# Second layer's attention of a two-layer decoder: scores in one run, projections in four parts, transposes and values in two shared PSUM banks

## Chip, cores and metric

The kernel runs on one core of a Trainium2 chip. The metric is the device time of one execution in microseconds (us), shown as the median of several runs. TensorE (PE) multiplies, with weight loads listed apart (PEld); VectorE (DVE) and ScalarE (ACT) read and write its results in PSUM, which has 8 banks of 2 KB a partition; SyncE (SP) and GpSimd (POOL) issue DMAs.

## What is computed

512 tokens of width 1024 go through two layers. The first mixes by a gated delta rule; the second, which the change touches, by attention over a sliding window of 128 tokens, with 12 query heads, 2 shared key/value heads of width 64 and a sink logit for each head. In both layers 4 further heads attend to 256 memory tokens. Then come the output projection and a gated feed-forward part (swiglu). Cut to the second layer:

```
h = rms_norm(x, ln_mix[layer])
proj = h @ swa_w_q[bl]                              # 1024 -> 768 + 256
q = apply_partial_rope(proj[..., :SWA_Q_W].reshape(b_sz, s_len, SWA_HEADS, SWA_DH), cos, sin)
mix_out = sliding_window_attention(q, shared_k, shared_v, swa_sinks[bl])
mem_q = proj[..., SWA_Q_W:]
mem_o = memory_attention(mem_q.reshape(b_sz, s_len, MEM_HEADS, MEM_DH), mem_k, mem_v)
x = x + jnp.concatenate([mix_out, mem_o], axis=-1) @ w_out[layer]
x = x + swiglu(rms_norm(x, ln_ffn[layer]), w_gate_up[layer], w_down[layer])

# in sliding_window_attention, over blocks of 128 queries and 2 x 128 keys:
m = jnp.maximum(jnp.max(s, axis=-1, keepdims=True), sink)
p = jnp.exp(s - m)
p = p / (jnp.sum(p, axis=-1, keepdims=True) + jnp.exp(sink - m))
o = jnp.einsum("bnhgqk,bnkhd->bnqhgd", p, vw)
```

## The kernel before

**Layout.** Activations lie transposed: 8 tiles of 128 features x 512 tokens. A projection (project, L198) makes one such tile from 8. Each operand is split into a high and a low part in fp32r (split, L165: hi by ScalarE, the rest lo by VectorE), and mm3 (L190) adds three products hi x hi, hi x lo, lo x hi for each of the 8 pieces k: 24 matmuls of 512 columns in one PSUM bank, all from L143, the helper line of every matmul. L137 is ScalarE's copy, L150 VectorE's tensor_tensor, L147 the transposes. weight (L179) loads a 128x1024 weight tile into wraw (2 buffers) and splits it into whi and wlo (3 buffers each).

**The second layer's attention** (swa, L1085). Query tiles 0 to 5 hold two heads each, on partitions 0 to 63 and 64 to 127; tiles 6 and 7 hold the four memory heads. A tile passes through these steps:
- queries(t): a projection, in a bank of pj, then a rotation by VectorE (rope, L1076) into q (3 buffers), or a product with rstd for tiles 6 and 7;
- scores (L723): for each of 4 query blocks n and both heads b, q times keys, on 64 rows of TensorE, into banks of qk. Two blocks share one qk buffer of two banks. VectorE adds the mask and takes the maximum into sm (L747), or for memory tiles takes the maximum (L751), and ScalarE writes the exponentials to sm. These fp32 matmuls appear as two instructions each in the profile, so that a tile has 16, in two halves of 8; so do the value matmuls;
- weigh (L759): for query tiles the sink and the exponentials first (L769 to L780), then the reciprocal of the sums, then for each block n: scaling (VectorE for even n, ScalarE for odd n), transposes into a bank of pt, a copy to pf or pfm (VectorE for n = 2, else ScalarE), and after the fourth block all products with the values into the bank sc, on 64 columns of TensorE;
- split (L825): that bank to the pair mix[t], h by ScalarE and l by VectorE.

PSUM in this stage has pj=2 banks, g=1, qk=1 buffer of two banks, pt=2, sc=1.

**Order.** swa writes out: queries 6 and 7, keys, values, scores of 6, the values' transposes, queries 0, scores of 7; then for t from 0 to 5 queries(t+1), scores of t, and weigh of the tile two behind; then weigh of 4 and 5. output (L828) follows: eight output tiles ("rows") m, each a projection over mix in the order k = 6, 7, 0, ..., 5, in banks pj, pj, g in turn, then by VectorE the addition to x (L837), a new pair of x times gain (L839: ScalarE, then VectorE) and a square for the next norm (L841).

A scheduler turns this into one list for each engine before the run: whenever an engine is free it takes the first instruction in program order whose inputs and buffers are ready by its own model of time, so that later instructions can be drawn ahead. nosync (L113) adds an order that costs no semaphore: the first transposes after a scores step stand behind its last matmul (L799), and the first value matmul behind the last transpose (L822). The list is fixed; on the chip each engine keeps to it and waits.

Of the kernel before, what the change touches and what calls it, by code (L numbers as in the profile page):

```python
# [18 lines left out]
P = 128  # L19
T = 512  # L20
D = 1024
KD = D // P
# [63 lines left out]
class Builder:  # L86
    def __init__(self, tc, a):
        self.tc, self.nc, self.a = tc, tc.nc, a
        self.n = 0
        self.table, self.table_ins, self.table_users = None, None, []  # L90


# [17 lines left out]
    def bank(self, tag, shape=(P, T)):  # L110
        return self.t(self.pp, list(shape), F32, tag, self.pbufs[tag])
# [114 lines left out]
    def build(self):  # L226
        tc, nc, a = self.tc, self.nc, self.a
        with ExitStack() as st:
            opened = lambda name, **kw: tc.tile_pool(name=name, bufs=1, reuse_waits="tile", **kw)
            pool = lambda name, **kw: st.enter_context(opened(name, **kw))  # L230
            cp = pool("const")
            self.wpool, self.apool = pool("w"), pool("acta")
            self.dpool = pool("scratch", space=DRAM)
            self.load_constants(cp)
            self.weng = nc.vector
            with opened("layer0", side="right") as self.mpool:
                with self.banks(pj=3, g=2, sc=3):
                    with opened("early", side="right") as ep:
                        self.mem_and_norm(ep)
                        self.gates(ep)  # L240
                    with opened("gdn", side="right") as gp:
                        mix = self.gdn(gp)
                    self.bpool, xp = pool("actb"), pool("x")
                    self.x = [self.t(xp, [P, T], F32, f"x{k}") for k in range(KD)]
                    for k in range(KD):
                        nc.sync.dma_start(self.x[k], a["xT"][:, k, :])
                    self.rstd, self.cosT, self.sinT = (self.t(xp, [P, T], F32, n) for n in ("rstd", "cosT", "sinT"))
                    h = self.output(xp, 0, mix, self.bpool)
            with opened("ffn0", side="right") as fp, self.banks(pj=2, g=6):
                self.ffn(fp, xp, 0, h, self.apool, rope=True)  # L250
            with self.banks(pj=2, g=1, qk=1, pt=2, sc=1):
                with opened("swa", side="right") as sp:
                    mix = self.swa(sp)
                h = self.output(xp, 1, mix, self.apool)
            with opened("ffn1", side="right") as fp, self.banks(pj=2, g=6):
                self.ffn(fp, xp, 1, h, self.bpool)

# [465 lines left out]
    def scores(self, pool, q, kk, win):  # L723

        nc = self.nc
        own = "pt" in self.pbufs
        half = [slice(0, 64), slice(64, P)]
        sm = [self.t(pool, [P, 2, 2, 2 * P], F32, "sm", 6 if own else 2) for _ in range(2)]
        sm = [t[:, n] for t in sm for n in range(2)]
        mx, den, nm = (self.t(pool, [P, 2 * NC], F32, t, 3 if own else 2) for t in ("mx", "den", "nm"))  # L730
        for n0 in range(0, NC, 2):
            if own:
                two = self.bank("qk", [P, 2, 2, 2 * P])
                ps = [two[:, b] for b in range(2)]
            else:
                ps = [self.bank("sc" if n0 else "g", [P, 2, 2 * P]) for _ in range(2)]
            for n in (n0, n0 + 1):
                ks = slice((n - 1) * P if n else 0, (n + 1) * P) if win else slice(0, ML)
                c0 = P if win and n == 0 else 0
                for b in range(2):  # L740
                    self.ahead = self.mm(ps[b][:, n - n0, c0:], q[half[b], n * P:(n + 1) * P], kk[half[b], ks])
            for b in range(2):
                i = b * NC + n0
                if win:
                    for n in (n0, n0 + 1):
                        c0 = 0 if n else P
                        nc.vector.tensor_tensor_reduce(  # L747
                            out=sm[n][:, b, c0:], in0=ps[b][:, n - n0, c0:], in1=self.band[:, c0:], scale=1.0,
                            scalar=NEG, op0=ALU.add, op1=ALU.max, accum_out=mx[:, b * NC + n:b * NC + n + 1])
                else:  # L750
                    nc.vector.tensor_reduce(out=mx[:, i:i + 2], in_=ps[b], op=ALU.max, axis=AX.X)  # L751
                    self.ts(nm[:, i:i + 2], mx[:, i:i + 2], -0.125, ALU.mult)
                    for n in (n0, n0 + 1):
                        i = b * NC + n
                        self.fn(sm[n][:, b, :], ps[b][:, n - n0, :], AF.Exp, scale=0.125, bias=nm[:, i:i + 1],
                                accum_out=den[:, i:i + 1])
        return sm, mx, den, nm

    def weigh(self, pool, scores, vv, m, out, sinks):  # L759

        nc = self.nc
        win = sinks is not None
        own = "pt" in self.pbufs
        half = [slice(0, 64), slice(64, P)]
        sm, mx, den, nm = scores
        if win:
            sk = sinks.unsqueeze(2).to_broadcast([P, 2, NC])
# [11 lines left out]
                            accum_out=den[:, i:i + 1])  # L779
            self.tt(nc.vector, den, den, es, ALU.add)  # L780
        nc.vector.reciprocal(den, den)
        o = self.bank("sc")
        group = NC if own else 2
        for n in range(NC):
            if n % group == 0:
# [22 lines left out]
            if own and n == 2:  # L808
                nc.vector.tensor_copy(to, pt[:, k0:])
            else:  # L810
                self.copy(to, pt[:, k0:])
            if (n + 1) % group:
                continue
            if win:
                parts = [(t[:, j, b, :], vv[n - 1 + j][:, half[b]], slice(n * P, (n + 1) * P), j if n else 0, j, b)
                         for n, t in pf.items() for j in range(0 if n else 1, 2) for b in range(2)]
            else:
                parts = [(pf[:, j, b, :], vv[j][:, m * P + 64 * b:m * P + 64 * b + 64],
                          slice((n + 1 - group) * P, (n + 1) * P), j, j, b) for j in range(2) for b in range(2)]
            for t, v, s, first, last, b in parts:  # L820
                ins = self.mm(o[half[b], s], v, t, first == 0, last == 1)
                if turned is not None:  # L822
                    self.nosync(ins, turned)
                    turned = None
        self.split(o, *out)  # L825


    def output(self, xp, layer, mix, hpool):  # L828

        nc, a = self.nc, self.a  # L830
        self.weng = nc.vector
        h = []
        self.acc = None
        for m in range(KD):
            ps = self.project(a["wout"][layer, m], mix, ("pj", "pj", "g")[m % 3],
                              (6, 7, 0, 1, 2, 3, 4, 5))
            self.tt(nc.vector, self.x[m], ps, self.x[m], ALU.add)  # L837
            hl = self.pair(hpool)
            self.split_gain(self.x[m], self.gain(G_FFN[layer], m), *hl)  # L839
            h.append(hl)  # L840
            self.acc = self.accumulate(xp, self.acc, self.x[m], m)  # L841
        return h
# [189 lines left out]

    def rstd_from(self, acc, t=slice(0, T)):
        self.use(LN_EXP)
        ps = self.bank("g")[:, t]
        self.mm(ps, self.ones, acc)
        self.rsqrt(self.rstd[:, t], ps, D)

# [46 lines left out]
    def swa(self, sp):  # L1085
        nc, a = self.nc, self.a
# [7 lines left out]
        kk, vv = [], []  # L1094

        def queries(t):
            ps = self.project(a["wq"][t], h)
            if len(qs) == 0:
                self.rstd_from(self.acc)
                for table in (self.cosT, self.sinT):  # L1100
# [16 lines left out]

        def transpose_values():
            v = vv.pop()
            pt = self.bank("g")  # L1120
            for c in range(NC):
                self.tr(pt[:, c * P:(c + 1) * P], v[:, c * P:(c + 1) * P])
            vt = self.t(sp, [P, NC, P], F32, "vt")
# [3 lines left out]
        def score(t):  # L1127
            got[t] = self.scores(sp, qs[t], kk[0] if t < 6 else memK[t - 6], t < 6)

        def weigh(t):  # L1130
            mix[t] = self.pair(self.bpool)
            if t < 6:
                self.weigh(sp, got[t], vv, t, mix[t], sinks[:, t, :])
            else:
                self.weigh(sp, got[t], memV, t - 6, mix[t], None)

        got = {}
        queries(6)
        queries(7)
        keys()  # L1140
        values()
        score(6)
        transpose_values()
        queries(0)
        score(7)

        behind = [6, 7]
        for t in range(6):
            if t < 5:
                queries(t + 1)  # L1150
            score(t)
            behind.append(t)
            weigh(behind.pop(0))
        for t in behind:
            weigh(t)
        return [mix[t] for t in range(KD)]

    def final(self, fp, squares, t):

# [84 lines left out]
```

## Time and profile before

| | |
|---|---|
| device time, median of 3 runs | 1167.67 us (1167.38 to 1167.92) |
| the profiled execution, its own time | 1167.76 us |
| its span, first to last instruction | 1165.5 us |
| mean granted TensorE clock | 0.998 |
| VectorE, ScalarE busy, whole span | 72%, 54% |
| DMA, mean | 130 GB/s, 151.20 MB |

All times are of one profiled execution, in us from its span's start. A timeline row holds start, duration, engine, line, operation, output<-inputs, shapes and count; equal neighbours are merged, so that "1.14 ... x8" are eight instructions from the first start to the last end. "64*128" means 64 rows and 128 columns of TensorE in use. A bracket gives the engine's idle time ahead and what ended it. Matmuls overlap, so a duration (0.39 for 512 columns) is longer than the distance between two starts, and TensorE counts as busy in between. A row of stretches holds the stretch, its length, the busy time and count of PE, PEld, DVE, ACT and POOL, the granted clock, the share of DMA and GB/s. A group row holds count | busy us, mean ns | idle us before, with who ended it.

The second layer's attention lies at about 660 to 775, its output rows behind it up to about 809.

### The profile page before, as it was taken

The numbers are of one execution on the slowest core, as the hardware profiler recorded it, in microseconds if no ns is written. First come the engines' busy times: TensorE is split into PE (matmuls) and PEld (weight loads), VectorE is DVE, ScalarE is ACT, GpSimd is POOL, SyncE is SP. The second block draws the span as 40 slices with busy tenths as digits, with TensorE's granted clock in tenths as the row PEclk, the third lists the DMA queues.
The fourth block names the chain that finished last, engine by engine and source line by source line (L and its number), as shares of the span: only waits on it lengthen the run. The fifth ranks groups of instructions, "written<-read, shape, count | busy, mean of one in ns | idle before, by whom it ended". The sixth has DMA issues, their size and how long they took to land.

```text
span 1165.5 us, 19274 instructions
## 1 busy us (share of the span) xinstructions
PE 1144.4 (98%) x7330; PEld 994.5 (85%) x7330; DVE 834.7 (72%) x1558; ACT 629.7 (54%) x1250; POOL 83.0 (7%) x93
## 2 busy tenths in 40 slices
PE   7999999999999999999999999999999999999997
PEld 5878777877899998899998876688999988999986
DVE  5664877767788877488966767758788734889644
ACT  7569663366466642266643546865566422566433
POOL 0210000000101101011100000010011000111000
PEclk9999999999999999999999999999999999999999
DMA  8334441224557636367623421144477633676232
GB/s 307 116 109 116 133 126 65 91 91 164 178 129 176 178 103 169 114 167 183 158 76 99 137 74 55 37 116 120 103 181 193 152 100 106 164 187 160 77 100 84
DMA packets 72943, 151.20 MB, mean 130 GB/s; under 512 B 16732, under 2 KB 19444, under 8 KB 72852
## 3 DMA queue, kind: packets, MB, share of 16 engines
q1 hardware_dynamic: 61908, 130.06, 35.3%
q0 software_dynamic: 10944, 19.93, 10.8%
q8 instruction: 57, 0.93, 0.3%
q14 instruction: 34, 0.28, 0.1%
HBM read 143.00 MB, written 6.96 MB: 129 GB/s over the span
## 4 chain that ended last, share of the span: by engine, by line
PE 90%; DVE 4%; ACT 3%; DMA 1%; issue 1%; SPq 0%; DVEq 0%; ACTq 0%
PE pj L143 43%; PE g L143 39%; PE sc L143 6%; ACT sm L131 1%; PE pt L147 1%; DVE wlo L150 1%; PE qk L143 1%; DVE big L150 1%; PE g L147 1%; DMA wraw<-in_wmk 1%; DVE btmp L150 1%; ACT sm L137 1%; DVE qv L153 1%; ACT whi L137 0%; DMA big<-basein 0%
## 5 line engine op out<-in xcount | busy, mean ns | idle before, releaser
L137 ACT ACTIVATE whi<-wraw 128x512 fp32r<-128x512 f32 (+3 forms) x325 | 243.0, 754 | 275.4 <-PE pj L143 173.5
L150 DVE TENSOR_TENSOR wlo<-wraw,whi 128x512 fp32r<-128x512 f32 (+3 forms) x325 | 272.5, 847 | 105.1 <-ACT whi L137 99.6
L143 PE MATMUL pj<-h,whi 128*128 128x512 f32 (+1 forms) x676 | 265.6, 394 | 0.2
L143 PE MATMUL pj<-l,whi 128*128 128x512 f32 (+1 forms) x676 | 265.2, 392 | 0.0
L143 PE MATMUL pj<-h,wlo 128*128 128x512 f32 (+1 forms) x676 | 264.1, 391 | 0.0
L143 PE MATMUL g<-T,whi 128*128 128x256 f32 x1216 | 220.5, 282 | 0.0
L143 PEld LDWEIGHTS g<-T,whi 128*128 128x128 f32 x1216 | 186.9, 189 | 1.1 <-DVE fu L153 1.1
L143 PE MATMUL g<-T,wlo 128*128 128x256 f32 x608 | 171.1, 281 | 0.0
L143 PE MATMUL g<-h,whi 128*128 128x256 f32 (+1 forms) x516 | 152.8, 296 | 0.0
L143 PE MATMUL g<-h,wlo 128*128 128x256 f32 (+1 forms) x516 | 152.0, 295 | 0.0
L143 PE MATMUL g<-l,whi 128*128 128x256 f32 (+1 forms) x516 | 151.8, 294 | 0.0
L143 PEld LDWEIGHTS pj<-h,whi 128*128 128x128 f32 x676 | 126.9, 188 | 28.9 <-issue 3.3
L143 PEld LDWEIGHTS pj<-h,wlo 128*128 128x128 f32 x676 | 127.1, 188 | 27.1 <-issue 1.9
L143 PEld LDWEIGHTS pj<-l,whi 128*128 128x128 f32 x676 | 127.1, 188 | 26.8 <-issue 1.4
L143 PEld LDWEIGHTS g<-T,wlo 128*128 128x128 f32 x608 | 114.4, 188 | 0.0
L143 PEld LDWEIGHTS g<-l,whi 128*128 128x128 f32 x516 | 97.9, 190 | 2.9 <-issue 0.5
L143 PEld LDWEIGHTS g<-h,whi 128*128 128x128 f32 x516 | 98.0, 190 | 2.9 <-issue 0.2
L143 PEld LDWEIGHTS g<-h,wlo 128*128 128x128 f32 x516 | 98.0, 190 | 2.4
L993 POOL DMA_DIRECT2D ws<-in_wgu x38 | 33.3, 876 | 740.0 <-DMA ws<-in_wgu 280.9
L137 ACT ACTIVATE whi<-ws 128x512 fp32r<-128x512 f32 x76 | 48.0, 631 | 49.5 <-PE g L143 41.2
L150 DVE TENSOR_TENSOR fu<-pj,rstd 128x512 f32<-128x512 f32 (+1 forms) x34 | 22.4, 660 | 53.7 <-PE pj L143 53.6
L150 DVE TENSOR_TENSOR wlo<-ws,whi 128x512 fp32r<-128x512 f32 x76 | 52.1, 686 | 7.3 <-ACT whi L137 7.2
(350 smaller groups left out, 1620.9 us busy)
## 6 DMA issues: line engine op xcount, KB each, us to landing
wraw<-in_wgu SPq DMA_DIRECT2D x50, 512.0 KB, 4.0
ws<-in_wgu SPq DMA_DIRECT2D x76, 256.0 KB, 3.4
ws<-in_wgu POOLq DMA_DIRECT2D x76, 256.0 KB, 4.7
wraw<-in_win SPq DMA_DIRECT2D x26, 512.0 KB, 3.7
wraw<-in_wdn SPq DMA_DIRECT2D x32, 384.0 KB, 3.1
wraw<-in_wdn SPq DMA_DIRECT2D x32, 320.0 KB, 2.9
wraw<-in_wgu SPq DMA_DIRECT2D x38, 256.0 KB, 4.1
wraw<-in_wout SPq DMA_DIRECT2D x16, 512.0 KB, 3.5
```

Of the source, the lines that this page charges most:

```text
L131: ins = self.nc.scalar.activation(out, in_, func, **kw).ins
L137: self.copied = self.nc.scalar.activation(out, in_, AF.Copy, **kw).ins
L143: return self.nc.tensor.matmul(out, lhsT, rhs, start=start, stop=stop, skip_group_check=more).ins
L147: return self.nc.tensor.transpose(out, in_, self.ident[:k, :k]).ins
L150: return eng.tensor_tensor(out=out, in0=a, in1=b, op=op).ins
L153: self.nc.vector.scalar_tensor_tensor(out=out, in0=in0, scalar=scalar, in1=in1, op0=op0, op1=op1)
L993: nc.gpsimd.dma_start(s1, a22, accum_op=ALU.add)
```

## The change

- PSUM in the stage becomes pj=2, qk=2 buffers of two banks, pt=2; g and sc are gone. The values' accumulator o, the bank of rstd_from, the transposed values and every third output row (from row 3 on) take pt. Output row 2 takes half of a qk buffer.
- weigh is cut in two: softmax (sink, exponentials, sums, reciprocal) and weighed, a generator that stops after blocks 1 and 3 of its transposes. The first score matmul of the next tile is ordered behind the last value matmul (valued).
- queries and the output rows become generators that stop after each k, three matmuls. beside runs two of them, blocks 0 and 1, two, blocks 2 and 3, two, and the values.
- The order becomes: queries 6, 7, scores of 6, keys, values, scores of 7, the values' transposes, queries 0, softmax 6, queries 1. Then for t from 0 to 5: scores of t; weigh of tile 6, 7, 0, 1, 2, 3 beside queries(t+2), for t = 4 and 5 beside the first four k of output rows 0 and 1; softmax of tile 7, 0, 1, 2, 3, 4. Then tile 4 beside more of rows 0, 1 and 2, softmax 5, and tile 5 beside one k of each. Only k = 5, the last of each row, is left to output, which now runs inside the pool swa.

```
-            with self.banks(pj=2, g=1, qk=1, pt=2, sc=1):
-                with opened("swa", side="right") as sp:
-                    mix = self.swa(sp)
-                h = self.output(xp, 1, mix, self.apool)
+            with self.banks(pj=2, qk=2, pt=2), opened("swa", side="right") as sp:
+                h = self.output(xp, 1, *self.swa(sp))
...
                     self.ahead = self.mm(ps[b][:, n - n0, c0:], q[half[b], n * P:(n + 1) * P], kk[half[b], ks])
+                    if self.valued is not None:
+                        self.nosync(self.ahead, self.valued)
+                        self.valued = None
...
     def weigh(self, pool, scores, vv, m, out, sinks):
+        self.softmax(pool, scores, sinks)
+        for _ in self.weighed(pool, scores, vv, m, out, sinks is not None):
+            pass
+
+    def softmax(self, pool, scores, sinks):
...
         nc.vector.reciprocal(den, den)
-        o = self.bank("sc")
+
+    def weighed(self, pool, scores, vv, m, out, win):
...
+        o = None if own else self.bank("sc")
...
+            if own and n % 2:
+                yield
             if (n + 1) % group:
                 continue
+            if own:
+                o = self.bank("pt")
...
+            self.valued = ins if own else None
         self.split(o, *out)
...
+    def row(self, layer, m, mix, bank):
+        w = self.weight(self.a["wout"][layer, m])
+        for n, k in enumerate((6, 7, 0, 1, 2, 3, 4, 5)):
+            if n:
+                yield
+            ps = bank() if n == 0 else ps
+            self.mm3(ps, w, k, mix[k], n == 0, n == KD - 1)
+        yield ps
+
+    def output(self, xp, layer, mix, begun=()):
...
+        hpool = self.apool if layer else self.bpool
+        bank = lambda m: self.bank(("pj", "pj", "pt" if begun else "g")[m % 3])
         for m in range(KD):
-            ps = self.project(a["wout"][layer, m], mix, ("pj", "pj", "g")[m % 3],
-                              (6, 7, 0, 1, 2, 3, 4, 5))
+            ps = list(begun[m] if m < len(begun) else self.row(layer, m, mix, lambda: bank(m)))[-1]
...
         def queries(t):
-            ps = self.project(a["wq"][t], h)
+            w = self.weight(a["wq"][t])
+            ps = self.bank("pj")
+            for k in range(KD):
+                self.mm3(ps, w, k, h[k], k == 0, k == KD - 1)
+                yield
...
+        def beside(t, work):
+            out = self.pair(self.bpool)
+            steps = self.weighed(sp, got[t], *((vv, t) if t < 6 else (memV, t - 6)), out, t < 6)
+            for _ in range(3):
+                for _ in range(2):
+                    next(work, None)
+                next(steps, None)
+            mix[t] = out
...
+        two = lambda: self.bank("qk", [P, 2, 2, 2 * P])[:, 0].rearrange("p a b -> p (a b)")
+        rows = [self.row(1, m, mix, (lambda: self.bank("pj")) if m < 2 else two) for m in range(3)]
+        some = lambda m, n: (next(rows[m]) for _ in range(n))
         got = {}
-        queries(6)
-        queries(7)
+        for t in (6, 7):
+            list(queries(t))
+        score(6)
         keys()
         values()
-        score(6)
+        score(7)
         transpose_values()
-        queries(0)
-        score(7)
-
-        behind = [6, 7]
+        list(queries(0))
+        softmax(6)
+        list(queries(1))
+
         for t in range(6):
-            if t < 5:
-                queries(t + 1)
             score(t)
-            behind.append(t)
-            weigh(behind.pop(0))
-        for t in behind:
-            weigh(t)
-        return [mix[t] for t in range(KD)]
+            work = queries(t + 2) if t < 4 else some(t - 4, 4)
+            beside((6, 7, 0, 1, 2, 3)[t], work)
+            list(work)
+            softmax((7, 0, 1, 2, 3, 4)[t])
+        work = all_of(some(0, 2), some(1, 2), some(2, 6))
+        beside(4, work)
+        softmax(5)
+        list(work)
+        beside(5, all_of(some(0, 1), some(1, 1), some(2, 1)))
+        return mix, rows
```

## The prediction on record

> **What bounds the kernel now.** I read the page first, then the stretches, the groups by form and the timelines of the second layer's attention.
>
> ```profile
> PE 1144.4 (98%) x7330; PEld 994.5 (85%) x7330; DVE 834.7 (72%) x1558; ACT 629.7 (54%) x1250; POOL 83.0 (7%) x93
> ```
>
> ```profile
> 680.75:782.15 101.40, 99.43 (x649) 72.45 (x649) 73.36 (x238) 72.17 (x212) 3.39 (x4) 1.00 0.20 59
> ```
>
> TensorE bounds it, 98% busy. The second row is the stage in question, from its first scores to the end of output row 2 (PE, PEld, DVE, ACT, POOL): PE 99.43 of 101.40 us, VectorE 73.36, ScalarE 72.17. So only TensorE's own time can be saved here. A busy PE is not a PE that streams, so I split its time by the distance between starts.
>
> ```profile
> 690.38 0.39 PE L143 MATMUL pj<-h,whi 128*128 128x512 f32 x1
> ```
>
> ```profile
> 692.88 0.39 PE L143 MATMUL pj<-h,wlo 128*128 128x512 f32 x1
> 693.20 1.14 PE L143 MATMUL qk<-mk,q 64*128 64x256 f32 x8
> 694.26 0.50 PE L143 MATMUL pj<-h,whi 128*128 128x512 f32 x1
> 694.60 0.40 PE L143 MATMUL pj<-l,whi 128*128 128x512 f32 x1
> ```
>
> ```profile
> 765.74 1.04 PE L147 MATMUL pt<-consts,sm 128*128 128x128 f32 x8
> 766.71 1.75 PE L143 MATMUL sc<-pf,vt 128*64 128x128 f32 x28
> 768.39 0.50 PE L143 MATMUL pj<-l,whi 128*128 128x512 f32 x1
> ```
>
> Projection matmuls (pj) start 2.50/11 = 0.227 us apart (eleven steps from 690.38 to 692.88): 24 take 5.45. Eight score matmuls (64 rows) last 1.14 and one alone about 0.39 (means in the groups below): (1.14-0.39)/7 = 0.107 each. But from pj at 692.88 to the second pj behind the run, 694.60, are 1.72 us, where two pj steps (0.454) and 8 x 0.107 (0.856) make 1.31. So **a run of scores costs 0.41 us over its work**, in steps of 0.32 instead of 0.227 before it, about 0.2 on the way out and 0.34 instead of 0.227 behind it. Likewise 28 value matmuls (64 columns): (1.75-0.28)/27 = 0.055 each, 1.53 in all, while the run takes 1.68; with about 0.07 in front and 0.1 behind, as at the scores, 0.32 over its work. Transposes cost (766.71-765.74)/8 = 0.12 each and nothing for the change to and from pj.
>
> ```profile
> L147 PE MATMUL pt<-consts,sm 128*128 128x128 f32 x116 | 16.7, 281 | 1.5 <-ACT pf L137 1.3
> L143 PE MATMUL qk<-ks,q 64*128 64x256 f32 x72 | 11.8, 396 | 0.0
> L143 PE MATMUL sc<-pf,vt 128*64 128x128 f32 x168 | 10.7, 277 | 0.0
> L143 PE MATMUL qk<-mk,q 64*128 64x256 f32 x32 | 4.5, 402 | 0.5 <-ACT sm L131 0.5
> L143 PE MATMUL sc<-pfm,mv 128*64 128x512 f32 x16 | 3.9, 605 | 0.0
> ```
>
> The stage's work: 9 projections (query tiles 0 to 5, output rows 0 to 2) x 5.45 = 49.0; 104 wide scores x 0.107 = 11.1; 24 half-wide ones (block 0 of a query tile has no predecessor: 4 of its 16) x 0.053 = 1.3; 120 transposes (116 and 4 of the values) x 0.12 = 14.4; 168 values x 0.055 = 9.2; 16 memory values in two runs, (3.9/2-0.6)/7 = 0.19 each, 3.1. Sum 88.1 of 101.4: **13.3 us are not work**. The PE timeline has 18 runs of scores (two of 8 for each of 8 tiles, two of them split 6 and 2) from the first row below to the second, 18 x 0.41 = 7.4, and 9 runs of values from the third to the one at 772.67 below, 2.9.
>
> ```profile
> 680.82 1.13 PE L143 MATMUL qk<-mk,q 64*128 64x256 f32 x8
> ```
>
> ```profile
> 758.91 1.14 PE L143 MATMUL qk<-ks,q 64*128 64x256 f32 x8
> ```
>
> ```profile
> 712.97 1.94 PE L143 MATMUL sc<-pfm,mv 128*64 128x512 f32 x8
> ```
>
> The other 3.0 is waiting. The last columns of the groups record 2.0 of it: 1.5 ahead of transposes, mostly for ScalarE's copy pf, and 0.5 ahead of the scores of tile 6. Once more from the timeline:
>
> ```profile
> 740.06 0.48 PE L143 MATMUL pj<-h,whi 128*128 128x512 f32 x1
> 741.01 1.14 PE L147 MATMUL pt<-consts,sm 128*128 128x128 f32 x8 [0.47 <-ACT pf L137]
> ```
>
> This shows why records understate: 0.95 us between starts where 0.227 is due, 0.47 of it recorded. A tile's third transposes wait there for a pt buffer, right behind the first two blocks.
>
> **The change part by part.**
>
> *Scores in one run.* The pool qk has two buffers instead of one, and a dependency keeps a tile's first score behind the last value matmul before it. The second eight no longer wait for the eviction of the first eight, so 8 runs of 16 stand for 18 runs: 10 x 0.41 = **4.1 us saved**. No run of 16 is in the trace. Bounds: 10 x 0.2 if the way in and out lengthens with the run, 10 x 0.41 if it doesn't; I take 0.41, since the way in and out belongs to the change of rows in use, which a second eight doesn't repeat. Behind the waiting score stand only matmuls of later steps; pj that are ready go ahead of it.
>
> *Projections in four parts.* Each tile is now 6 pj, transposes of blocks 0 and 1, 6 pj, blocks 2 and 3, 6 pj, values, 6 pj. The 6 pj (1.36 us) stand between a pt buffer's filling and its reuse, and the copy that frees it takes 0.69 at most (at 772.34 below): the 1.5 us of pt waits go. The qk wait goes with the second buffer. With the unrecorded rest **3.0 saved**; at the least 2.0. Values become 8 runs: **0.3**.
>
> *Values in pt.* The accumulator sc is gone; values take whichever pt buffer is free first, that of block 2, copied by VectorE. Query tiles 0 to 3 leave 6 pj as cover, beside tiles 2 and 3 nothing stands there, but output-row matmuls are ready to be drawn forward. The weighing tile's result leaves pt long before its buffer is needed again (a run of scores, 1.9 us, and 12 pj later). For these **0.8 lost**: between 0, all drawn forward, and 1.6, with 0.45 (worked out below) for tiles 2 and 3 and 0.1 for each of seven others' waits of one VectorE operation; nearer to neither.
>
> If instead the gap of 0.47 recorded above returned in each of eight tiles, 3.8 would be lost here (rival 2). The Trainium skill, page Perfetto Trace Analysis (Identifying Performance Opportunities), says that a gap which keeps returning on the engine that should be saturated can mean too little PSUM for the next tile; by that rule the pt waits, which agree, would grow, as transposes and values together get one buffer fewer.
>
> *Loads.* Rows 0 to 2 are loaded and split from the loop, not after it.
>
> ```profile
> 700.46 50.98 SPq L176 DMA_DIRECT2D wraw<-in_wout  x5
> ```
>
> Five output loads are issued by 751.44 already, 30 us ahead of use, so SP's queue costs nothing; POOL issues nothing here. The instruction counts on ScalarE and VectorE stay: 72 and 73 us in a stage of 98, beside TensorE's work.
>
> *The end, which is new.* Before, output row 2 was hardly begun when tile 5's values ended, and its 24 matmuls hid everything. Now rows 0, 1 and 2 stand complete but for k=5, and nothing else is ready.
>
> ```profile
> 771.70 1.04 PE L147 MATMUL pt<-consts,sm 128*128 128x128 f32 x8
> 772.67 1.75 PE L143 MATMUL sc<-pf,vt 128*64 128x128 f32 x28
> 774.35 0.50 PE L143 MATMUL pj<-h,wlo 128*128 128x512 f32 x1
> ```
>
> ```profile
> 776.30 0.39 PE L143 MATMUL pj<-h,wlo 128*128 128x512 f32 x1
> ```
>
> ```profile
> 772.34 0.69 DVE L809 COPY pf<-pt 128x512 f32<-128x512 f32 x1 [1.32 <-PE pt L147]
> ```
>
> ```profile
> 775.10 0.69 DVE L150 TENSOR_TENSOR l<-sc,h 128x512 fp32r<-128x512 f32 x1 [1.99 <-ACT h L137]
> 776.73 1.29 DVE L150 TENSOR_TENSOR x<-pj,x 128x512 f32<-128x512 f32 x2 [0.94 <-PE pj L143]
> 777.93 1.22 DVE L150 TENSOR_TENSOR wlo<-wraw,whi 128x1024 fp32r<-128x1024 f32 x1
> ```
>
> ```profile
> 774.46 0.60 ACT L137 ACTIVATE h<-sc 128x512 fp32r<-128x512 f32 x1 [1.09 <-PE sc L143]
> 776.50 2.01 ACT L137 ACTIVATE whi<-wraw 128x1024 fp32r<-128x1024 f32 x2 [1.43 <-PE pj L143]
> ```
>
> (a) Values took sc 0.97 after the first transpose at 771.70; in pt they wait for the copy of block 2, which ends at 773.03: with a hop, 0.45 later. (b) PE is free at 774.35; h ends at 775.06, l at 775.79. Three first matmuls (0.68) fill between the two: 0.7 + 0.1 = 0.8; 1.3 if the rows go strictly one by one. (c) Row 3 needs a whi/wlo pair, and rows 0 to 2 hold all three. Call the start of row 0's last matmul r (776.30 here): whi follows at 0.2, wlo ended at r+2.85 behind two additions. From r PE has 5 x 0.227 = 1.13 for rows 0 to 2 and 0.45 for row 3's first two matmuls: 2.95-1.58 = 1.4 idle. Row 2's addition (0.6), whose result comes earlier now, goes ahead of wlo: 2.0. With all the evictions ahead (two more operations of 0.65) 3.3. I take 2.0. **End: 0.45 + 0.8 + 2.0 = 3.3 lost** (2.65 to 5.0).
>
> **Sum.** 4.1 + 3.0 + 0.3 - 0.8 - 3.3 = 3.3 us saved. The profiled execution took 1167.76 us (span 1165.5 and 2.26 around it), 0.09 above the median 1167.67: span 1162.2, **1164.4 us** against the median.
>
> **The rivals.**
>
> 1. *The end is longer.* 5.0 there: 7.4-0.8-5.0 = 1.6 saved, **1166.1**. For it: evictions come first in program order. Against it: at 776.50 ScalarE did whi twice ahead of the evictions.
>
> 2. *A gap at pt in every tile.* 7.4-3.8-3.3 = 0.3 saved, **1167.4**. For it: one buffer fewer, and the values need a buffer that VectorE frees. Against it: 1.36 us of pj now stand at both places, twice a copy.
>
> 3. *The idle end slows TensorE's clock.* The kernel's start shows a slow pace:
>
> ```profile
> 6.78 0.58 PE L143 MATMUL pj<-mh,whi 128*128 128x256 f32 x1 [6.78 <-ACT whi L137]
> ```
>
> ```profile
> 10.64 0.39 PE L143 MATMUL pj<-mh,whi 128*128 128x256 f32 x1
> 10.86 0.29 PE L143 MATMUL pj<-ml,whi 128*128 128x256 f32 x1
> 10.98 0.28 PE L143 MATMUL pj<-mh,wlo 128*128 128x256 f32 x1
> ```
>
> Equal matmuls start 0.21 apart up to 10.86 and 0.12 apart from there; the kernel's first started 4.1 earlier. Another such phase costs up to 4.1 x (1-0.12/0.21) = 1.8: with rival 1, 0.2 lost, **1167.9**. Against it: the gaps of 0.5 in this stage slowed nothing, and 5 us here come in three pieces with work between. The Trainium skill, TensorE: Matmul & The Clock Gate (Part 1), gives this rule: an idle window of about 3.4 us halves the clock. The start agrees; no later gap in this trace is long enough to test it.
>
> 4. *The change doesn't do what it says:* the scheduler draws pj or waits into the run of 16, so 18 entries remain. 7.4-4.1-0.8-3.3: 0.8 lost, **1168.5**. For it: the trace has runs split 6 and 2. Against it: the split was at a run waiting for values, which now come first.
>
> 5. *Slower: softmax behind the values.* In program order softmax of the next tile now follows h, the copy of the value product.
>
> ```profile
> 743.05 0.40 ACT L131 ACTIVATE sm<-sm,nm 128x128 f32<-128x128 f32 x1 [0.27 <-DVE nm L157]
> ```
>
> ```profile
> 743.93 0.49 ACT L131 ACTIVATE sm<-sm,nm 128x256 f32<-128x256 f32 x1
> ```
>
> ```profile
> 744.44 0.60 ACT L137 ACTIVATE h<-sc 128x512 fp32r<-128x512 f32 x1
> ```
>
> ```profile
> 759.06 0.17 DVE L150 TENSOR_TENSOR den<-den,es 128x8 f32<-128x8 f32 x1 [0.67 <-ACT sm L131]
> ```
>
> ```profile
> 759.50 1.01 DVE L157 TENSOR_SCALAR sm<-sm,den 128x128 f32<-128x128 f32 x4
> ```
>
> If ScalarE kept that order, its eight exponentials (six of 0.49, two of 0.40, 3.8 in all) would start 0.6 after the values and end at 4.4; VectorE adds 0.44 to the first scaling, two scalings of 0.25 and a hop, 1.1: transposes at 5.5, while TensorE has 6 pj, 16 scores and 6 pj, 4.7. At 0.85 for six tiles, 5.1: 1.8 lost, **1169.5**. It decides from 0.55 a tile (3.3/6). Against it: already now the next tile's exponentials (743.05, 743.93) go ahead of this tile's h (744.44), though written behind it.
>
> 6. *Short end.* 2.65, and nothing in the body: 4.75 saved, **1162.9**.
>
> **How the numbers follow.** Forecast 0.43 (own range 1163.4 to 1166.0: waits of 2.0 to 3.0 and row 3's weights at 1.4 to 2.6), longer end 0.15, pt gap 0.10, clock 0.05, unmerged 0.07, softmax 0.12, short end 0.08. 0.2% is 2.34 us, about what a measurement of this kernel tells from no change: below 1165.33 or above 1170.0. Faster: 0.34 of the forecast, 0.08 of the short end, 0.05 of the longer: 0.47. Slower: 0.07 of softmax, 0.03 of the others: 0.10. Within: 0.43. The range 1163.0 to 1168.8 leaves out half of the short end (0.04) and some 0.13 above.
>
> **What would show it.** Runs qk x16, with 0.32 before and 0.34 behind them (else step 1 fails); no recorded pt wait in tiles 0 to 3 (else step 2); a gap on PE ahead of tile 5's values, one behind them, and one at row 3 released by wlo (steps a, b, c); no softmax release ahead of transposes (else rival 5). A gap above 1 us inside the loop, or an end above 5 us, makes the prediction wrong.

## The result, and the profile after

The changed kernel took 1168.71 us (median of 21 runs, 1166.77 to 1171.27), the kernel before 1167.67 beside it (21 runs): a ratio of 1.0009, 95% interval 1.0002 to 1.0015. Measured a second time it took 1167.86 against 1167.94, 1.0003 (0.9995 to 1.0011). So no gain can be measured, and a loss is 0.15% at most by these intervals; 1164.4 was forecast. The profiled execution took 1168.72 us, its span 1166.9, the granted clock 0.997.

From its page, the busy times of the engines:

```profile
PE 1140.4 (98%) x7330; PEld 994.3 (85%) x7330; DVE 833.5 (71%) x1558; ACT 630.5 (54%) x1250; POOL 83.1 (7%) x93
```

TensorE is busy 4.0 us less than before (1144.4) and the span is no shorter: what was saved came back as idle time. To see where, I cut both profiles at two matmuls that exist in both, the sums for rstd (they read sqa) ahead of the attention and ahead of the feed-forward part. Each row of stretches runs from the one to the other, first for the kernel before:

```profile
663.53:814.84 151.31, 149.34 (x867) 113.20 (x866) 109.56 (x293) 92.12 (x237) 3.52 (x4) 1.00 0.28 86
```

and for the changed kernel, in its first profile and in a second one:

```profile
664.82:815.84 151.02, 145.56 (x867) 113.02 (x865) 106.78 (x289) 92.04 (x237) 3.49 (x4) 1.00 0.29 83
```

```profile
662.63:813.51 150.88, 145.51 (x867) 113.25 (x866) 107.44 (x291) 91.83 (x237) 3.51 (x4) 1.00 0.30 85
```

The first number is the stretch's length, the second TensorE's busy time; their difference is its **idle time: 1.97 us before (1.93 in a second profile), 5.46 and 5.37 after**. Busy time fell by 3.8 to 3.9, idle time rose by 3.5, and the stretch is 0.3 to 0.5 shorter. (In the four profiles of the two kernels it starts anywhere between 662.6 and 664.8, behind code that is the same in both. That the medians' difference of 1 us, and its vanishing in the second measurement, come from there too is likely, but a median has no profile to show it. The length of this stretch repeats within 0.15 in the two profiles of each kernel, so I compare lengths.)

The groups of the stage, by form (count | busy, mean ns | idle ahead, and what ended it):

```profile
L148 PE MATMUL pt<-consts,sm 128*128 128x128 f32 x116 | 15.6, 272 | 0.0
L144 PE MATMUL pt<-pf,vt 128*64 128x128 f32 x168 | 10.5, 276 | 2.9 <-DVE pf L822 2.9
L144 PE MATMUL qk<-ks,q 64*128 64x256 f32 x72 | 8.8, 376 | 0.0
```

The wide scores of the query tiles cost 8.8 in place of 11.8 and the transposes wait no longer (1.5 before): steps 1 and 2 of the change work. But the query tiles' values, which had waited for nothing, now wait 2.9 us for pf, VectorE's copy of block 2. One run of scores and one such wait, in the timeline of TensorE:

```profile
732.19 0.39 PE L144 MATMUL pj<-h,wlo 128*128 128x512 f32 x1
732.51 1.79 PE L144 MATMUL qk<-ks,q 64*128 64x128 f32 x16
734.23 0.50 PE L144 MATMUL pj<-h,whi 128*128 128x512 f32 x1
734.56 0.39 PE L144 MATMUL pj<-l,whi 128*128 128x512 f32 x1
```

```profile
737.76 1.03 PE L148 MATMUL pt<-consts,sm 128*128 128x128 f32 x8
...
739.79 0.40 PE L144 MATMUL pj<-h,wlo 128*128 128x512 f32 x1
740.83 1.75 PE L144 MATMUL pt<-pf,vt 128*64 128x128 f32 x28 [0.64 <-DVE pf L822]
```

The run of 16 has 0.32 ahead and 0.33 behind, once. Block 2's four transposes end at about 738.4, block 3's at 738.8, and six projection matmuls (1.36) stand behind them as planned. What VectorE does meanwhile:

```profile
737.89 0.42 DVE L750 CUSTOM_DVE_ANT_0 sm<-qk,consts 128x256 f32<-128x256 f32 x1
...
738.32 1.22 DVE L151 TENSOR_TENSOR wlo<-wraw,whi 128x1024 fp32r<-128x1024 f32 x1
739.45 0.20 DVE L787 RECIPROCAL den<-den 128x8 f32<-128x8 f32 x1
...
739.69 0.48 DVE L158 TENSOR_SCALAR sm<-sm,den 128x128 f32<-128x128 f32 x2
740.09 0.68 DVE L822 COPY pf<-pt 128x512 f32<-128x512 f32 x1
```

VectorE is busy without a break. It has just masked the whole run of scores (the last of eight at 737.89), and its fixed list puts the next weight's wlo, the reciprocal and two scalings ahead of block 2's copy. That copy starts 1.7 us after its transposes have ended. It ends at 740.77, and the values start at 740.83, ahead of the end of block 3's copy (741.14): by the program their first matmul reads block 0, copied long before, and what it waits for is the bank that block 2's copy frees. Block 3's copy, on ScalarE, stands behind scalings that wait for the same part of VectorE's list:

```profile
739.75 0.91 ACT L138 ACTIVATE sm<-sm,den 128x256 f32<-128x256 f32 x2 [2.51 <-DVE mx L154]
740.56 0.58 ACT L138 ACTIVATE pf<-pt 128x512 f32<-128x512 f32 x1
```

The values wait for block 2's copy in tiles 1, 2 and 3: 0.64, 1.15 and 0.73 (in tile 3 no wlo stands ahead of it, but the masks, the reciprocal and four scalings do). In the memory tiles 6 and 7, whose values read the one tile pfm that all four copies write, they wait 0.38 and 0.49 for the last copy, ScalarE's and VectorE's. Together this is **3.4 us**; the 2.9 of the group holds 0.35 of tile 5 besides, which is counted with the end below.

In the kernel before, tile 1's copy stood behind a wlo (739.54) and four masks too, and this cost nothing: the values had the bank sc and started beside the copy.

```profile
742.05 0.69 DVE L809 COPY pf<-pt 128x512 f32<-128x512 f32 x1
```

```profile
742.07 0.88 PE L143 MATMUL sc<-pf,vt 128*64 128x128 f32 x12
```

So in the query tiles two things come together: a late copy, and a bank that values and transposes share. The end, in TensorE's timeline:

```profile
776.90 1.75 PE L144 MATMUL pt<-pf,vt 128*64 128x128 f32 x28 [0.35 <-DVE pf L822]
779.35 0.74 PE L144 MATMUL pj<-h,whi 128*128 128x512 f32 x2 [0.70 <-ACT h L138]
...
782.68 0.50 PE L144 MATMUL pj<-h,whi 128*128 128x512 f32 x1 [0.21 <-ACT whi L138]
...
783.93 0.50 PE L144 MATMUL pj<-h,wlo 128*128 128x512 f32 x1 [0.52 <-DVE wlo L151]
```

Waits (a), (b) and (c) are all there and come to **1.8 us**. With 0.24 ahead of tile 0's scores (for q) this makes 5.4 of the 5.46.

### The profile page after: what moved, and what is told of

It is laid out like the page before. It is cut to its first block, busy times and chain, and to the rows that moved or that the text cites. A ratio compares the mean times of both kernels' runs of the same rounds, so it can differ in the third digit from the quotient of the medians.

```text
span 1166.9 us, 19281 instructions
## 1 busy us (share of the span) xinstructions
PE 1140.4 (98%) x7330; PEld 994.3 (85%) x7330; DVE 833.5 (71%) x1558; ACT 630.5 (54%) x1250; POOL 83.1 (7%) x93
## 4 chain that ended last, share of the span: by engine, by line
PE 82%; DVE 10%; ACT 5%; DMA 1%; issue 1%; SPq 0%; DVEq 0%; ACTq 0%
PE pj L144 39%; PE g L144 38%; PE sc L144 4%; DVE wlo L151 2%; ACT sm L132 2%; DVE sm L750 1%; PE pt L144 1%; DVE big L151 1%; ACT whi L138 1%; DVE btmp L151 1%; PE g L148 1%; DMA wraw<-in_wmk 1%; ACT sm L138 1%; DVE q L151 1%; DVE qv L154 1%
## 5 line engine op out<-in xcount | busy, mean ns | idle before, releaser
L144 PE MATMUL g<-h,whi 128*128 128x256 f32 (+1 forms) x500 | 146.6, 293 | 0.0
L144 PE MATMUL g<-h,wlo 128*128 128x256 f32 (+1 forms) x500 | 145.8, 292 | 0.0
L144 PE MATMUL g<-l,whi 128*128 128x256 f32 (+1 forms) x500 | 145.5, 291 | 0.0
L144 PEld LDWEIGHTS g<-h,whi 128*128 128x128 f32 x500 | 94.9, 190 | 2.3 <-issue 0.5
L144 PEld LDWEIGHTS g<-l,whi 128*128 128x128 f32 x500 | 94.9, 190 | 2.3 <-issue 0.5
L144 PEld LDWEIGHTS g<-h,wlo 128*128 128x128 f32 x500 | 95.0, 190 | 1.8
```

Source lines behind the costliest of these rows:

```text
L144: return self.nc.tensor.matmul(out, lhsT, rhs, start=start, stop=stop, skip_group_check=more).ins
```

## The experiments

Theories: **Q**, the values wait because block 2's and 3's copies stand too far back in VectorE's and ScalarE's queues; **S**, they wait because values and transposes share two banks; **E**, the end's waits are want of work there. Each run was timed beside the kernel before. Idle is that of the stretch between the two rstd sums.

| run | median us | ratio to before (95%) | stretch | PE busy | idle |
|---|---|---|---|---|---|
| before, again | 1168.07 | 1.0000 (0.9992 to 1.0009) | 151.35 | 149.42 | 1.93 |
| after, again | 1167.86 | 1.0003 (0.9995 to 1.0011) | 150.88 | 145.51 | 5.37 |
| copy_first | 1167.75 | 0.9998 (0.9989 to 1.0007) | 150.51 | 146.38 | 4.13 |
| copy_act | 1168.84 | 1.0006 (0.9997 to 1.0015) | 151.63 | 145.79 | 5.84 |
| split_scores | 1167.40 | 0.9997 (0.9988 to 1.0006) | 150.57 | 147.48 | 3.09 |
| row3 | 1170.88 | 1.0026 (1.0015 to 1.0036) | 155.11 | 147.57 | 7.54 |
| late_forced | 1167.33 | 0.9994 (0.9985 to 1.0003) | 150.56 | 145.24 | 5.32 |
| own_bank | 1170.56 | 1.0022 (1.0014 to 1.0031) | 153.40 | 146.48 | 6.92 |
| hold2 | 1166.26 | 0.9985 (0.9976 to 0.9994) | 148.81 | 145.22 | 3.59 |
| split_first | 1166.45 | 0.9986 (0.9977 to 0.9994) | 149.83 | 148.02 | 1.81 |
| split_first_hold | 1164.26 | 0.9968 (0.9956 to 0.9980) | 148.01 | 147.83 | 0.18 |
| three_first_hold | 1162.79 | 0.9953 (0.9942 to 0.9965) | 146.22 | 144.94 | 1.28 |

**Both kernels once more** (after_again, before_again), no edit.

> The changed kernel once more, unaltered. In its first profile the changed stage was 0.2 us shorter than in before's, but the first 1000 matmuls, whose code is the same, took 184.1 us against 183.0. Theory H (that head differs from execution to execution): its head comes out somewhere between 182 and 184.5, the stage again 180.3, the median 1168.0 to 1168.8. Theory P (the head goes with the program): the head is 184.0 again, and the median 1168.7.

> The kernel before once more, unaltered. Theory H: a head between 182 and 184.5, the stage again 180.5, the median 1167.8. Theory P: a head of 183.0 again.

Measured: the lengths of the stretch stay (151.3, 150.9), its start does not: 664.82 and 662.63 us in two executions of the changed kernel. H holds for the head; the changed kernel's median, 1167.86, came out 0.14 below the range that H gave.

**copy_first**: the same instructions in another order. moved holds the copies of blocks 2 and 3; wlo and den stand behind the first on VectorE, the scalings of the next tile's block 1 behind the second on ScalarE.

```
+    def behind(self, ins, i):
+        if self.moved[i] is not None:
+            self.nosync(ins, self.moved[i])
...
+            self.behind(self.split(raw[:, s], hi[:, s], lo[:, s], eng or self.weng), 0)
...
+            self.behind(self.tt(nc.vector, den, den, es, ALU.add), 0)
...
+                    if own and n == 1:
+                        self.behind(self.copied, 1)
```

> The changed kernel with one thing altered: the copies of blocks 2 and 3 out of pt are ordered, on VectorE and on ScalarE, ahead of the next weight's wlo and of the next tile's den and scalings. Same instructions, same banks. Theory Q (the values wait because block 2's copy stands behind wlo, 1.22 us, and the small ones in VectorE's queue): the waits of 0.4 to 1.2 us ahead of the values of tiles 6, 7, 1, 2 and 3 fall to 0.3 or less each, some 3 us go, 1165.5 (1165.0 to 1166.5). Theory S (the two shared banks themselves make them wait): the waits stay, 1168.7. Theory W (wlo, now 0.7 to 2 us later, makes the next tile's projection wait): the same 3 us come back there, 1168 to 1170.

Measured: 1167.75, idle 4.13. In tile 2 VectorE now has the copy ahead of wlo (first fence). The second has the two longest entries of TensorE's waits in the stage (us in total, times, longest).

```profile
748.93 0.68 DVE L829 COPY pf<-pt 128x512 f32<-128x512 f32 x1
...
749.60 1.22 DVE L152 TENSOR_TENSOR wlo<-wraw,whi 128x1024 fp32r<-128x1024 f32 x1
```

```profile
PE pt L145 <- DVE pf L829: 1.3, 2, 1.0
PE pj L145 <- ACT h L139: 1.1, 2, 0.7
```

The waits of tiles 1 and 3 for pf are gone. 1.0 stays in tile 2, where the copy still stands behind all eight masks. So the order counts, as Q says, but the idle time falls by 1.3 only, and the median misses Q's range (1165.0 to 1166.5): wlo is one part of what stands ahead of the copy, the masks are the other. TensorE's busy time is 0.8 higher besides. Part of this can be seen: tile 1's run of values lasts 2.01 in place of 1.75, and tile 4's comes in two pieces.

**copy_act**: block 2's copy on ScalarE.

```
-            if own and n == 2:
+            if False:
```

> The changed kernel with block 2's copy on ScalarE in place of VectorE, nothing ordered by hand. ScalarE has that copy and block 3's behind a scaling of the next tile, which waits for the reciprocal, which stands behind wlo on VectorE. Theory Q (the place in the queues decides): the values still come as late, 0.1 to 0.2 us saved a tile, 1167.7 to 1168.7. Theory L (VectorE has too much work in a tile, 0.64 us less of it is enough): the waits go, 1165.5. Theory S (shared banks): 1168.7.

Measured: 1168.84, idle 5.84. VectorE has 4.8 us less to do in the stretch (101.94 for 106.78 in the row below against the changed kernel's) and TensorE waits no less. In tile 1 ScalarE begins the copy at 740.25, behind a scaling that had waited 2.53 for VectorE. It is not VectorE's load, but what stands ahead of the copy. L falls; between Q and S this run does not decide.

```profile
664.80:816.43 151.63, 145.79 (x868) 112.85 (x866) 101.94 (x281) 95.33 (x245) 3.49 (x4) 1.00 0.29 83
```

**split_scores**: the window tiles' scores in two runs again.

```
+            if between is not None and n0:
+                next(between, None)
             for n in (n0, n0 + 1):
...
-            score(t)
             work = queries(t + 2) if t < 4 else some(t - 4, 4)
+            score(t, work)
```

> The changed kernel with each of the six window tiles' scores in two runs again, one step of the projection between them: six more entries into 64-row runs. If an entry costs 0.41 us as the profile of before has it (4.1 us for ten, the first term of the sum), 6 x 0.41 = 2.5 us are lost, 1171.2 (1170.5 to 1171.8). If the merging is worth nothing: 1168.7. If the second half of the scores a step later takes load off VectorE at the transposes: a few tenths less than 1171.2, and the waits ahead of the values change.

Measured: 1167.40. Five tiles got two runs (in the sixth no step stood between), and both halves of the trade are in the table: busy time rose by 147.48 - 145.56 = 1.92, 0.38 for each of five runs, which confirms the price; idle time fell by 2.37. I had not seen that. In tile 1 VectorE's list is the same as in the changed kernel, and counted from the first score matmul (732.51 there, 731.91 here) the copy is hardly earlier:

```profile
738.28 1.03 PE L148 MATMUL pt<-consts,sm 128*128 128x128 f32 x8
```

```profile
739.37 0.69 DVE L824 COPY pf<-pt 128x512 f32<-128x512 f32 x1
```

The copy starts 7.46 us behind the first score (7.58 in the changed kernel). But the transposes of blocks 2 and 3 start 6.37 behind it (5.25): a step of the projection and the price of an entry now lie between. **What the merged run did is bring transposes and values 1.1 us nearer to the scores**, while VectorE needs as long as before to get through its eight masks and what follows.

**split_first**: both edits.

> The kernel with the scores in two runs, and in it the copies of blocks 2 and 3 ordered ahead of wlo, den and the scalings as well. If both act on the same waits (theory Q: the run of scores and the order both decide when VectorE gets to block 2's copy), only the remaining 0.8 us at the values of tiles 6, 7, 2 and 3 can go: 1166.6 (1166.2 to 1167.2). If they act on different things, 1.3 and 1.0 add up: 1166.4 from 1168.7. If splitting helps for another reason than VectorE's queue, nothing more is gained: 1167.4.

Measured: 1166.45, which fits both of the first two forecasts; the list of waits says more. All that TensorE still waits for:

```profile
PE pj L145 <- ACT h L139: 0.7, 1, 0.7
PE pj L145 <- DVE wlo L152: 0.5, 1, 0.5
PE pt L145 <- DVE pf L831: 0.3, 1, 0.3
PE pj L145 <- ACT whi L139: 0.2, 1, 0.2
```

These are the end's four (0.3 for tile 5's values among them). In the body there is **no wait left, and the two banks are shared as before**: sharing alone does not make the values wait, and S falls as it was put. In tile 1 VectorE now has the masks behind it and waits for the transposes itself:

```profile
737.90 0.69 DVE L831 COPY pf<-pt 128x512 f32<-128x512 f32 x1 [0.70 <-PE pt L149]
```

**own_bank**: a bank for the values alone, one for the transposes.

```
-            with self.banks(pj=2, qk=2, pt=2), opened("swa", side="right") as sp:
+            with self.banks(pj=2, qk=2, pt=1, sc=1), opened("swa", side="right") as sp:
...
-            if own and n % 2:
+            if own:
                 yield
...
-            for _ in range(3):
-                for _ in range(2):
+            for n in (2, 2, 1, 1, 1):
+                for _ in range(n):
```

> The changed kernel with a bank of their own for the values (sc), which leaves the transposes one bank: each block's transposes wait for the copy of the block before, with one to two steps of the projection between. The order then puts the values behind all eight steps. Theory S (sharing banks is what makes the values wait): no wait ahead of the values, small ones of 0.1 to 0.3 at the transposes, 1166.0. Theory Q (VectorE's queue): block 3's transposes wait for block 2's copy, which is as late as before, 0.5 to 1.2 us in tiles 1, 2 and 3, and the values, later, do not: 1167.5 to 1170.

Measured: 1170.56, a little beyond what Q allowed, and S is 4.6 off. The query tiles' values wait no longer, and the transposes (L148) do:

```profile
PE pt L148 <- DVE pf L822: 2.0, 3, 0.8
PE pt L148 <- ACT pf L138: 2.0, 2, 1.2
```

Block 2's copy is as late as before and is waited for in tiles 1, 2 and 5. The other 2.0 are the price of one bank for the transposes: in tile 3 block 1's wait for the copy of block 0, in tile 5 block 2's for that of block 1. So the run shows that the late copy costs as much elsewhere, but not what a third bank would do: the eight are taken (2 + 4 + 2), and no run had one more.

**late_forced**: the values behind eight steps.

```
-            for _ in range(3):
-                for _ in range(2):
+            for n in (2, 2, 4):
+                for _ in range(n):
...
                     self.nosync(ins, turned)
+                    if own:
+                        self.nosync(ins, self.last)
```

> The changed kernel with each tile's values behind all eight steps of the projection instead of six, held there by an order. Theory Q (the values wait for block 2's and 3's copies, which stand in the queues of VectorE and ScalarE): two steps more, 1.36 us, cover the 0.46, 0.57 and 0.72 of tiles 6, 7 and 1, and four returns to the projection between values and scores go, 0.2 each; tiles 2 and 3, which have only four steps of a row, keep their 2.0: 2.5 us less, 1166.2 (1165.7 to 1166.8). Theory S (the shared banks): the values' bank comes free later as well, and the next tile's transposes wait for l instead, 0.3 to 0.5 a tile: 1168 to 1169.

Measured: 1167.33, a miss; idle 5.32 as before.

```profile
PE pt L148 <- ACT pf L138: 1.7, 3, 0.9
PE pt L144 <- DVE pf L822: 1.1, 2, 0.8
```

The values of tiles 6, 7, 1 and 3 wait no longer, but the transposes of blocks 2 and 3 now wait for ScalarE's copies of the first blocks, 1.7 in three places, and once, 0.45, for l, as S had it. The order moved more than the values: in tile 1 those copies start 2.65 us behind the first transposes (736.22 and 733.57), 0.48 in the changed kernel (736.20 and 735.72), behind four scalings. More cover at one consumer didn't help, as the new list put other copies further back; between Q and S this run does not decide.

**row3** and **hold2**, the end. In row3 a fourth row is begun, from weight tiles of its own; in hold2 steps of row 2 are held back.

```
+        rows.append(self.row(1, 3, mix, two, pool=sp, tags=("w3h", "w3l"), bufs=1))
...
+        list(some(3, 7))
         return mix, rows
```

> The changed kernel with row 3 of the output's projection begun too: its weight in two tiles of its own, seven of its eight steps behind tile 5's values, while h and l of tile 5 are made. Theory E (the end's waits are for want of work: 0.8 for h, 0.4 and 0.7 for row 3's whi and wlo): some 1.5 us go, 1167.2 (1166.8 to 1167.7). Rival: row 4's weights, whose buffers come free only when row 0 ends, wait in place of row 3's, and only the 0.8 goes: 1168.0 to 1168.6.

```
-        work = all_of(some(0, 2), some(1, 2), some(2, 6))
+        work = all_of(some(0, 2), some(1, 2), some(2, 2))
...
-        beside(5, all_of(some(0, 1), some(1, 1), some(2, 1)))
+        beside(5, all_of(some(0, 1), some(1, 1), some(2, 2)))
+        list(some(2, 3))
```

> The changed kernel with less of row 2 ahead of tile 5's transposes, two steps of it ahead of tile 5's values and two behind them. Theory E (the 0.8 us for tile 5's h is for want of work): 1.36 us of work stand there, the 0.8 goes, 1167.9 (1167.5 to 1168.2). Rival: tile 5's values, which now come sooner after their transposes, wait 0.5 to 1.0 for block 2's and 3's copies: 1168.5 to 1169.0.

Measured: hold2 1166.26, better than E said, as the waits for h, whi, wlo and tile 5's pf all went. Its whole list is the body's:

```profile
PE pt L144 <- DVE pf L822: 2.4, 3, 1.1
PE pt L144 <- DVE nm L158: 0.5, 1, 0.5
PE pt L144 <- ACT pfm L138: 0.4, 1, 0.4
PE qk L144 <- DVE q L151: 0.2, 1, 0.2
```

row3 has no wait at that place either, but was slower, 1170.88: rows 4 to 7 and the feed-forward's start came in another order on VectorE, and the last row's addition to x came late:

```profile
809.80 0.76 PE L144 MATMUL pj<-h,whi 128*128 128x512 f32 x1 [4.31 <-DVE x L151]
810.37 0.63 PE L144 MATMUL pj<-l,whi 128*128 128x512 f32 x1
```

Neither E nor its rival had this; why the order changed so was not looked into further.

**split_first_hold** and **three_first_hold**: split_first with hold2's end; and copy_first's order with hold2's end, the scores in one run and three steps, not two, ahead of the first transposes (the cut shows this last part).

```
-            for _ in range(3):
-                for _ in range(2):
+            for n in (3, 2, 2):
+                for _ in range(n):
```

> The kernel with the scores in two runs and the copies ordered first (no waits in the body), with the end of the run with row 2 held back as well. If the body's waits and the end's are separate, the two gains add up: 1.3 and 2.3 us of the stage, 1168.7 - 3.6 = 1165.1 by the changed kernel's median, 1164.2 by the median of the run with row 2 held back: 1164.6 (1164.0 to 1165.2). If the end's gain was only the body's lateness moved, 1166.0 or more.

> The changed kernel with the scores in one run but three steps of the projection, not two, ahead of the first transposes (one is left behind the values), the copies ordered first and row 2 held back. Theory Q: one step, 0.68 us, more between a tile's scores and the values gives VectorE the time that splitting gave it, without the 0.41 of each split (five of them, 2.1 us): 1162.7 (1162.0 to 1163.5). If 0.68 us is too little, waits of 0.3 to 1.2 us come back at the values of tiles 6, 7, 2 and 3: 1164 to 1165.

Measured: 1164.26 for the first, with 0.18 idle in the whole stretch, so the two causes are separate and together all of it; and for the second **1162.79, 0.47% below the kernel before (ratio 0.9953, 0.9942 to 0.9965)** and faster than the changed one, as Q had it. The step that gives VectorE its time costs nothing when it stands between scores and transposes: TensorE's busy time is 144.94, against 147.83 with split scores. Tile 1 there, VectorE and TensorE:

```profile
735.91 0.68 DVE L829 COPY pf<-pt 128x512 f32<-128x512 f32 x1
736.59 1.22 DVE L152 TENSOR_TENSOR wlo<-wraw,whi 128x1024 fp32r<-128x1024 f32 x1
```

```profile
737.60 1.75 PE L145 MATMUL pt<-pf,vt 128*64 128x128 f32 x28
```

The copy ends at 736.6, a microsecond before the values start, and wlo comes behind it. Two waits are left, at tiles 2 and 3, where only four steps of a row stand beside the tile:

```profile
PE pt L145 <- DVE pf L829: 0.7, 1, 0.7
PE pt L149 <- ACT pf L139: 0.5, 1, 0.5
```

## Why the prediction was wrong

- **Scores in one run, and one run of values fewer: 4.4 forecast, 3.8 to 3.9 measured** as busy time. The price of a run, 0.41, was measured again at 1.92/5 = 0.38 (split_scores). Nearly right; rival 4 is out.
- **The waits at pt and qk: 3.0 forecast, 2.0 measured.** All idle time of before (1.97) went, no transposes wait. The "unrecorded rest" of 1.0, which I took from distances between starts, did not come back as a gain. Why is open: the new waits carry a like rest (739.79 to 740.83 is 1.04, of which 0.227 was due and 0.64 is recorded, so 0.17 is not). The lower end of the term (2.0) was its value.
- **Values in pt: 0.8 forecast, 3.4 measured (bound 1.6). This is the step that failed.** The values do take block 2's bank, as the term says. But it counted the cover, six matmuls or 1.36 us, against a copy of 0.69 that starts when its transposes are done, and did not ask where in VectorE's list the copy stands. In tile 1 it started 1.7 us later than that, behind masks, wlo, reciprocal and scalings, and in tile 2 the gap above 1 us appeared (1.15) that was named as a sign of a wrong prediction. The views were at hand: VectorE was 73 us busy of 101, and in before the same copy stands behind a wlo and four masks; it cost nothing there because the values had a bank of their own. With the copy ordered first and the scores split the 3.4 vanish (split_first), with the banks as they are. Rival 2 had the place, nearly the size (3.8 in all eight tiles; it was five) and with the shared banks half of the reason; the half that it lacked is the late copy. The rule that stood beside it (the Trainium skill, Perfetto Trace Analysis, Identifying Performance Opportunities) says that such gaps can mean too little PSUM. This case agrees in part: in the kernel before the values had a bank of their own and did not wait; but they can do without it, as split_first shows.
- **The end: 3.3 forecast, 1.8 measured**, in the three places named: 0.35 for 0.45, 0.70 for 0.8, 0.73 for 2.0. Term (c) was mis-sized. Taken away, the end gave 2.1 to 2.2 of the stretch (hold2: 148.81 against 150.88 and 151.02).
- **Softmax behind the values** (rival 5): no transposes wait for an exponential. It didn't happen.
- **Sum**: 3.8 + 2.0 - 3.4 - 0.2 - 1.8 = 0.4 saved (0.2 is the wait for q at tile 0), against 0.3 and 0.5 in the stretch; forecast 3.3. The end, 1.5 better than forecast, hides part of the miss. That the first median lies just inside the stated range of 1163.0 to 1168.8 is luck, not support for the terms.

## What to carry to other kernels

When a run of matmuls is merged or moved, look at what it hands to the next engine. That engine needs as long as before for it, while the matmuls that follow the run come sooner; whatever stands behind that work in the engine's fixed list can then be late for them, however short it is. Here a bank that two uses share turned such a late copy into a wait. Cover has to be counted from the moment at which the queue reaches an instruction, not from the moment at which its data are ready. Where two versions differ by less than the scatter, compare a stretch between two matmuls that both have, and its busy and idle time apart.

## What the runs showed besides

**The clock after an idle stretch.** Behind the 4.31 us of row3 matmuls start 0.427 apart instead of 0.227, thirteen of them up to 815.06, some 2.6 us lost. The row of stretches gives the granted clock as 0.50:

```profile
810.00:813.00 3.00, 3.00 (x8) 2.32 (x9) 3.00 (x6) 1.05 (x3) 0.00 (x0) 0.50 0.29 55
```

This is rival 3's mechanism, and the rule cited there (the Trainium skill, TensorE: Matmul & The Clock Gate, Part 1: a window of about 3.4 us without work halves the clock) agrees; that page of the Trainium skill gives 426.7 ns between such starts at the low clock, the trace 427. The changed kernel's waits, 1.15 at the longest, slowed nothing: its stretch has a clock of 1.00.

**The same code in two executions.** Of the 1.3 us by which the changed kernel's stretch began later in the first two profiles, 1.0 arose in the first layer, at a product of qv and kn (two times eight matmuls) that waited in one execution and not in the other; the kernel before, then the changed one:

```profile
154.79 2.21 PE L143 MATMUL g<-qv,kn 128*128 128x128 f32 x16
```

```profile
155.02 1.05 PE L144 MATMUL g<-qv,kn 128*128 128x128 f32 x8
157.10 1.16 PE L144 MATMUL g<-qv,kn 128*128 128x128 f32 x8 [1.03 <-ACT qv L132]
```

In the second profiles the wait is 0.41 in the kernel before and 0.27 in the changed one, so it differs from one execution of the same kernel to the next. What decides its length was not tried.
